# A hybrid decoder step with a mixture of experts: the first expert pair's tokens picked by products of high and low parts of x's rows, kept where the last three weight slots are loaded

## The chip, the cores and the metric

The kernel runs on one core of a Trainium2 chip. The metric is the device time of one execution in microseconds (us); lower is better. Times of several executions are compared by their median.

## The reference, cut to what matters

One layer of a decoder is computed for 256 prompt tokens and 32 sample tokens (8 sequences of 4), so 288 rows of 1024 numbers in float32. Two attention branches and an output projection give new rows `x`; then each row goes through a mixture of 16 experts, of which it uses two:

```python
g_prob = softmax(xn @ w_rg + b_rg); g_p, g_i = top_k(g_prob, 1)
e_logit = (xn @ w_re + b_re).reshape(B, T, 4, 4)          # only the chosen group's 4
e_p, e_i = top_k(softmax(e_logit[g_i]), 2)
w_sel = g_p * e_p / sum(e_p); ids = g_i * 4 + e_i
y = sum over the two experts: w_sel * (silu(xn @ w_gate[e]) * (xn @ w_up[e])) @ w_down[e]
x = x + y; return rms_norm(x, g_final), and the new keys and values
```

## The kernel before, in words

The change lies between the output projection and the experts. The rows of x leave the projection transposed (`xT`, 8 tiles of 128 columns by 288 tokens). `back` adds each tile's part to the router's logits and to the sums of squares in one PSUM bank (`lgp`). `natural(t, c)` (L796) turns token tile t (of 128, 128 and 32 rows), column half c, back into rows: four TensorE transposes into a PSUM bank and one copy into `x2`. `rows_out` writes `x2` to the DRAM tensor `x2_d`, from which POOL later gathers the rows of each expert pair.

VectorE then finds each row's group and two experts (L904 to L926). `cums`, a product with a triangle of ones, numbers the rows of each expert, and `posm` (L939) holds those numbers. An expert has 64 slots, so two experts, a pair, fill 128 slots, and there are eight pairs. One-hot matrices (`oh0` in float32 for pair 0, `onehot` in bfloat16 for pairs 1 to 7) say which row stands in which slot. For pairs 1 to 7 a small product gives row indices (`index_mm`, `index`), and `fetch` gathers the rows from `x2_d` by an indirect DMA. For pair 0 no gather is made: `pick(c)` (L978) multiplies `oh0` with the rows of x2 in SBUF, in float32, which gives `xe0`. `turn_xe` transposes it into `xeT`, scaled by the norm's weights, and the first `gu` product (L1154, gate and up weights) starts. Beside this the same stretch computes row scales for pair 0 (`rsl`, L1022), the combine weights (`cw`), and, inside pair 0's products, `late_router` and `slot_weights`.

The weights of the experts come as 48 loads of 1 MB into a ring of 19 slots in four pools (8, 5, 3 and 3 slots); the loads' order is fixed by `use` (L819). Load n goes to slot n modulo 19. Loads 0 to 15 are issued by SP during the projections. Loads 16 to 18 go to the fourth pool, `rings[3]`, which is allocated when the projection's memory is free: load 16 is issued ahead of the second `rows_out`, loads 17 and 18 behind it (L896 to L903). Load 19 needs slot 0, which the first products of pair 0 set free; from then on each load waits for the products that use the slot's last content. SP issues all of these in program order. Each pair p needs its `gu` products for k from 0 to 3, then k from 4 to 7, and its `pd` products (L1202). The order on PE is written out by a small driver with costs; ACT and VectorE run this stretch in program order (`hold`, L891).

Of the kernel before, what the change touches and what calls it, by code (L numbers as in the profile page):

```python
# [17 lines left out]
D = 1024  # L18
# [103 lines left out]
def build(tc, I, O):  # L122
# [21 lines left out]
    def P(tag, name):  # L144
        return ps.tile([128, 512], F32, tag=tag, name=name, bufs=NBUF[tag])
# [647 lines left out]
            mm(lgp[:n, 72 + t:73 + t], sx[:, t * 128:t * 128 + n], ones[:, 0:1], start=False, stop=last,  # L793
               skip_group_check=True)

    def natural(t, c, copy=nc.scalar.copy):  # L796

        n = TW[t]
        pb = P("at", f"bk{t}{c}")
        for k in range(4):  # L800
            nc.tensor.transpose(pb[:n, k * 128:(k + 1) * 128], xT[c][:, k, t * 128:t * 128 + n], ident)
        copy(x2[:n, t, c * 512:(c + 1) * 512], pb[:n])

    def back(dt, xt, sx):
        if dt == 7:
            natural(0, 0, V.tensor_copy)
            sum_squares(rb, False)
        for t in range(3):
            n = TW[t]
            mm(lgp[:n, t * 24:(t + 1) * 24], xt[:, t * 128:t * 128 + n], wro[:, dt, :], start=(dt == 0 and t == 0),  # L810
               stop=(dt == 7), skip_group_check=True)
        if dt == 7:
            sum_squares(sx, True)
        yield 400.0, 0.0
# [78 lines left out]
    nc.scalar.activation(x2[:, 0:2, D], lgp[:, 72:74], AF.Ln, bias=epst, scale=1.0 / D)  # L893
    nc.scalar.activation(x2[0:32, 2, D:D + 1], lgp[0:32, 74:75], AF.Ln, bias=epst[0:32], scale=1.0 / D)
    nc.scalar.activation(x2[:, :, D], x2[:, :, D], AF.Exp, scale=-0.5)
    for c in range(2):  # L896
        for t in range(c == 0, 3):
            natural(t, c)
        if c:
            ring_loads(1)  # L900
        last = rows_out(slice(c * 512, c * 516 + 512))
    with tc.issue_after(last.ins):
        ring_loads(RINGS[3] - 1)  # L903
    for t in range(3):  # L904
        n = TW[t]
        V.scalar_tensor_tensor(lg[:n, t, :], lgp[:n, t * 24:(t + 1) * 24], x2[:n, t, D:D + 1], br[:n],
# [32 lines left out]
    V.scalar_tensor_tensor(posm, cums[:, 0:48].rearrange("p (t e) -> p t e", e=16), 1.0, OHs, op0=ALU.add, op1=ALU.mult)  # L939


    oh0 = mo.tile([128, 3, 2, CAP], F32, tag="PT", name="oh0", bufs=2)
    onehot = [mo.tile([128, 16, CAP], BF16, tag="y" + "hhl"[t], name=f"oneh{t}", bufs=2) for t in range(3)]
    inv = wk.tile([128, 8], I32, name="inv")
    invf = wk.tile([128, 8], F32, name="invf")
# [8 lines left out]
                        cc("io64")[:, None, :].broadcast_to([128, e1 - e0, CAP]), op=ALU.is_equal)  # L954

    def slots_of(t, pr):
        if pr == 0:
            return oh0[:TW[t], t].rearrange("p e s -> p (e s)")
        return onehot[t][:TW[t], 2 * pr:2 * pr + 2, :].rearrange("p e s -> p (e s)")

    def index_mm(p0, p1):
        for pr in range(p0, p1):
            for t in range(3):
                mm(piv[:, pr, :], slots_of(t, pr), (tokb if pr else tokf)[:TW[t], t, :], start=(t == 0), stop=(t == 2))

    def index(p0, p1):
        rs = slice(p0, p1)
# [7 lines left out]
                                            bounds_check=NT - 1, oob_is_err=False)  # L975


    def pick(c):  # L978
        po = P("at", f"xe0{c}")
        cs = slice(c * 512, c * 512 + 512)  # L980
        for t in range(3):
            mm(po, slots_of(t, 0), x2[:TW[t], t, cs], start=(t == 0), stop=(t == 2))
        (nc.scalar.copy, V.tensor_copy)[c](xe0[:, cs], po)

    def turn_xe(xeT, xe, pr):

        xv = xe[:, 0:D].rearrange("t (p k) -> t k p", k=8)
        for kk in range(2):
            pv = P("at", f"xe{pr}{kk}").rearrange("p (k t) -> p k t", k=4)
            for k in range(4):  # L990
                nc.tensor.transpose(pv[:, k, :], xv[:, 4 * kk + k, :], ident)  # L991
            ks = slice(4 * kk, 4 * kk + 4)
            i = V.tensor_mul(xeT[:, ks, :], pv, gpk[:, ks, None].broadcast_to([128, 4, 128]))  # L993
        return i

    for t in range(3):
        V.tensor_tensor(oh0[:, t], posm[:, t, 0:2, None].broadcast_to([128, 2, CAP]),
                        cc("io64")[:, None, :].broadcast_to([128, 2, CAP]), op=ALU.is_equal)
    for t in range(3):
        mark(t, 2, 6)  # L1000


    ge, gs, ee, es, w2, s4 = s3("ge", 4), s3("gs"), s3("ee", 2), s3("es"), s3("w2", 2), s3("s4")
# [14 lines left out]
    V.reciprocal(gs, gs)  # L1018
    V.reciprocal(s4, s4)
    V.tensor_tensor(ee, ee, bc(s4[:, :, None], 2), op=ALU.mult)  # L1020
    for t in range(3):
        mm(pi[:, 16:17], slots_of(t, 0), x2[:TW[t], t, D:D + 1], start=(t == 0), stop=(t == 2))  # L1022
    xe0 = gt.tile([128, 4 * NT], F32, tag="xT", name="xe0")
    pick(0)
    index_mm(0, 3)
    index(0, 3)
    fetch(1)
    fetch(2)
    pick(1)
    xeTs[0] = gt.tile([128, 4 * NT], F32, tag="xT", name="xeT0")[:, 0:D].rearrange("p (k t) -> p k t", k=8)  # L1030
    rsl[0] = mo.tile([128, 1], F32, tag="rsl", name="rsl0", bufs=3)
    V.tensor_copy(rsl[0], pi[:, 16:17])
    turn_xe(xeTs[0], xe0, 0)
    V.tensor_reduce(es, ee, axis=AX.X, op=ALU.add)
    V.reciprocal(es, es)
    V.tensor_tensor(ee, ee, bc(gs[:, :, None], 2), op=ALU.mult)
# [4 lines left out]
    for t in range(3):  # L1041
        mark(t, 6, 16)
# [5 lines left out]
    def late_router():  # L1048
        for t in range(3):
# [94 lines left out]
    def up(pr):  # L1144
        pt = P("mm", f"gu{pr}")
        if pr == 6:
            gfb.append(ring_slot(52, "gfb")[:, 0:D])
            nc.sync.dma_start(gfb[0], I["g_final"][None, :].broadcast_to([128, D]))
        for k in range(8):
            if pr == 7 and k == 0:  # L1150
                add_rows(1)
                add_rows(0)
            for i in range(2):
                mm(pt[64 * i:64 * i + 64, :], xeTs[pr][:, k, 64 * i:64 * i + 64], W[pr, k // 4, i][:, :, k % 4, :],  # L1154
                   start=(k == 0), stop=(k == 7))
            if pr == 0 and k == 4:
# [5 lines left out]
            if pr == 0 and k == 7:  # L1162
# [204 lines left out]
```

## Time and profile before

| what | value |
| --- | --- |
| time, median of 3 runs | 415.95 us (412.25 to 420.18) |
| time of the profiled execution | 413.99 us, of which 412.2 us span |
| mean granted TensorE clock | 0.989 |
| busy PE, VectorE, ACT, POOL | 95%, 50%, 44%, 23% |
| moved by DMA | 111.12 MB, mean 270 GB/s |

The span is the time from the first to the last instruction; about 1.8 us of the execution lie outside. PE is shown busy nearly always, but a matmul's end is modelled, so that share does not tell how close PE is to its limit. The chain of waits follows the work that ended last back to its causes. DMA share is the mean busy share of 16 DMA engines; GB/s is what they moved.

### The profile page before, as it was taken

The numbers are of one execution on the slowest core, as the hardware profiler recorded it, in microseconds if no ns is written. First come the engines' busy times: TensorE is split into PE (matmuls) and PEld (weight loads), VectorE is DVE, ScalarE is ACT, GpSimd is POOL, SyncE is SP. The second block draws the span as 40 slices with busy tenths as digits, with TensorE's granted clock in tenths as the row PEclk, the third lists the DMA queues.
The fourth block names the chain that finished last, engine by engine and source line by source line (L and its number), as shares of the span: only waits on it lengthen the run. The fifth ranks groups of instructions, "written<-read, shape, count | busy, mean of one in ns | idle before, by whom it ended". The sixth has DMA issues, their size and how long they took to land.

```text
span 412.2 us, 7107 instructions
## 1 busy us (share of the span) xinstructions
PE 393.2 (95%) x2706; PEld 293.5 (71%) x2706; DVE 207.9 (50%) x435; ACT 179.6 (44%) x349; POOL 94.3 (23%) x127
## 2 busy tenths in 40 slices
PE   7899999999999999999999999998999999999990
PEld 4799988858987977997999999984543333333350
DVE  3964468556543647134647785244540111126874
ACT  4854358577653664674554446232001111112353
POOL 3730222105343320610000232331002222033011
PEclk9999999999999999999999999999899999999997
DMA  8998636635743963663899999939599999999903
GB/s 263 327 355 277 222 103 230 223 118 205 260 158 91 338 235 103 220 240 103 192 381 395 341 324 389 409 88 303 189 313 413 410 416 412 417 414 410 343 32 122
DMA packets 56777, 111.12 MB, mean 270 GB/s; under 512 B 7621, under 2 KB 36941, under 8 KB 54689
## 3 DMA queue, kind: packets, MB, share of 16 engines
q1 hardware_dynamic: 49312, 86.56, 59.6%
q0 software_dynamic: 7120, 23.95, 15.8%
q8 instruction: 23, 0.38, 0.4%
q10 hardware_dynamic: 304, 0.09, 0.1%
q14 instruction: 18, 0.14, 0.1%
HBM read 104.72 MB, written 7.43 MB: 272 GB/s over the span
## 4 chain that ended last, share of the span: by engine, by line
PE 69%; DMA 20%; ACT 3%; issue 2%; DVE 2%; POOL 1%; SPq 1%; DVEq 0%; POOLq 0%
DMA w<-in_w_expert_up 15%; PE g L347 10%; PE g L351 10%; PE g L348 10%; DMA w<-in_w_expert_down 6%; PE gu L1154 4%; PE pk L616 3%; PE p L347 2%; PE p L348 2%; PE p L351 2%; PE ss L622 2%; PE o L347 2%; PE pos L647 2%; PE pd L1202 2%; PE po L588 2%
## 5 line engine op out<-in xcount | busy, mean ns | idle before, releaser
L347 PE MATMUL g<-xTh,hi 128*128 128x288 f32 x312 | 90.7, 311 | 0.0
L348 PE MATMUL g<-xTl,hi 128*128 128x288 f32 x312 | 85.7, 296 | 0.0
L1154 PE MATMUL gu<-w,xeT 128*64 128x512 f32 x256 | 62.0, 612 | 1.1 <-DMA w<-in_w_expert_up 0.7
L347 PEld LDWEIGHTS g<-xTh,hi 128*128 128x128 f32 x312 | 58.7, 188 | 1.0 <-issue 0.9
L348 PEld LDWEIGHTS g<-xTl,hi 128*128 128x128 f32 x312 | 58.9, 189 | 0.0
L351 PE MATMUL g<-xTh,li 128*128 128x288 f32 x312 | 50.5, 300 | 0.0
L333 DVE TENSOR_TENSOR li<-rawi,hi 128x1024 fp32r<-128x1024 f32 x39 | 47.3, 1215 | 3.0 <-ACT hi L328 3.0
L328 ACT CAST hi<-rawi 128x1024 fp32r<-128x1024 f32 x39 | 40.8, 1049 | 15.2 <-PE g L348 15.1
L351 PEld LDWEIGHTS g<-xTh,li 128*128 128x128 f32 x312 | 43.8, 189 | 1.7 <-issue 1.7
L1154 PEld LDWEIGHTS gu<-w,xeT 128*64 128x64 f32 x256 | 18.7, 139 | 33.1 <-issue 31.4
L1202 PE MATMUL pd<-w,hT 128*64 128x512 f32 x128 | 29.2, 598 | 0.0
L993 DVE TENSOR_TENSOR xeT<-xe,gpk 128x512 f32<-128x512 f32 x16 | 10.4, 686 | 22.9 <-PE xe L991 22.9
L617 ACT COPY KT<-pk 128x512 f32<-128x512 f32 x30 | 18.6, 639 | 7.1 <-PE pk L616 6.7
L1172 DVE SCALAR_TENSOR_TENSOR h<-gu,rsl,h 128x256 f32<-128x256 f32 x8 | 3.9, 484 | 34.3 <-ACT h L1169 34.3
L973 POOL DMA_INDIRECT xe<-x_d,inv x7 | 7.3, 1041 | 56.7 <-DVE rsl L1141 26.2
L1169 ACT ACTIVATE h<-gu,rsl 128x256 f32<-128x256 f32 x8 | 3.8, 474 | 37.5 <-PE gu L1154 19.8
L1202 PEld LDWEIGHTS pd<-w,hT 128*64 128x64 f32 x128 | 8.6, 136 | 15.4 <-issue 13.7
L616 PE MATMUL pk<-blob,kp 128*128 128x128 f32 x128 | 19.4, 274 | 0.1
L505 DVE TENSOR_TENSOR gate<-g,rb 128x288 f32<-128x288 f32 x16 | 7.3, 457 | 21.3 <-PE g L351 21.1
L347 PE MATMUL p<-oTh,hp 128*128 128x288 f32 x64 | 17.5, 296 | 0.0
L348 PE MATMUL p<-oTl,hp 128*128 128x288 f32 x64 | 17.4, 294 | 0.0
L1212 ACT COPY y<-pd 128x512 f32<-128x512 f32 x10 | 5.9, 586 | 23.6 <-PE pd L1202 23.6
(301 smaller groups left out, 708.6 us busy)
## 6 DMA issues: line engine op xcount, KB each, us to landing
rawi<-in_w_in SPq DMA_DIRECT2D x19, 1024.0 KB
w<-in_w_expert_gate SPq DMA_DIRECT2D x32, 512.0 KB
w<-in_w_expert_up SPq DMA_DIRECT2D x32, 512.0 KB
w<-in_w_expert_down SPq DMA_DIRECT2D x16, 1024.0 KB
rawo<-in_w_out SPq DMA_DIRECT2D x4, 1024.0 KB
y_d<-y POOLq DMA_DIRECT2D x10, 256.0 KB, 9.6
rawp<-in_w_proj_sb SPq DMA_DIRECT2D x2, 1024.0 KB
rawp<-in_w_proj_moba SPq DMA_DIRECT2D x2, 1024.0 KB
```

The costliest lines, as they stand in the source:

```text
L328: nc.scalar.copy(h, src)
L333: V.tensor_sub(l, src, h.bitcast(F32))
L347: mm(o, h[:, k, :], mh[k], start=(k == 0), stop=False)
L348: mm(o, h[:, k, :], ml[k], start=False, stop=False)
L351: mm(o, l[:, k, :], mh[k], start=False, stop=(k == n - 1))
L588: mm(po[64 * s:64 * s + 64, 128 * c:256], vn[:, c, h * 64:(h + 1) * 64], aT[s][:, 256 * c:256 + 128 * c], start=(c == 0), stop=(c == 1))
L616: nc.tensor.transpose(pv[:, j, :], kp[:, c, j * 128:(j + 1) * 128], ident)
L617: nc.any.tensor_copy(kt[:, :, c:256:2], pv)
L622: mm(pt[32 * bb:32 * bb + 32, 0:260], Qb[:, j, 4 * G + bb, :, :].rearrange("p h q -> p (h q)"), KT[bb][:, j, :], start=(j == 0), stop=(j = ...
L993: i = V.tensor_mul(xeT[:, ks, :], pv, gpk[:, ks, None].broadcast_to([128, 4, 128]))
L1154: mm(pt[64 * i:64 * i + 64, :], xeTs[pr][:, k, 64 * i:64 * i + 64], W[pr, k // 4, i][:, :, k % 4, :], start=(k == 0), stop=(k == 7))
L1202: mm(pd[64 * i:64 * i + 64, :], hT[:, k, 64 * i:64 * i + 64], W[pr, 2, i][:, k, c * 512:(c + 1) * 512], start=(k == 0), stop=(k == 1))
```

## The change

The rows of x are stored twice more for pair 0's pick: a high part (a cast to fp32r, `xsp[t][:, 0]`) and a low part (row minus high part, `xsp[t][:, 1]`). These three tiles take the three slots of `rings[3]`, so loads 16 to 18 are issued behind the last product that reads them. `pick` becomes six fp32r products per column half in place of three in float32. The first `natural` moves from VectorE to ACT and behind the logits; ACT writes two copies for each. The low parts are computed by POOL for column half 0, by VectorE for half 1. Pair 0's indices are no longer computed, its row scales move into `late_router`, the one-hot matrices of pairs 3 to 7 are computed ahead of the combine weights, `late_router` moves from k = 4 to k = 5 of pair 0, and `slot_weights` from pair 0 to pair 1.

```diff
+        nc.scalar.copy(xsp[t][:n, 0, cs], pb[:n])
+        nc.scalar.copy(x2[:n, t, cs], pb[:n])
+
+    def natural_low(t, c, eng):
...
+        eng.tensor_sub(xsp[t][:n, 1, cs], x2[:n, t, cs], xsp[t][:n, 0, cs].bitcast(F32))
...
         if dt == 7:
-            natural(0, 0, V.tensor_copy)
             sum_squares(rb, False)
...
+    xsp = [rings[3].tile([128, 2, D], F32R, tag="w", name=f"xsp{t}") for t in range(3)]
     for c in range(2):
-        for t in range(c == 0, 3):
+        for t in range(3):
             natural(t, c)
-        if c:
-            ring_loads(1)
-        last = rows_out(slice(c * 512, c * 516 + 512))
-    with tc.issue_after(last.ins):
-        ring_loads(RINGS[3] - 1)
+            if c == 0:
+                natural_low(t, c, nc.gpsimd)
+        rows_out(slice(c * 512, c * 516 + 512))
...
     def pick(c):
         po = P("at", f"xe0{c}")
         cs = slice(c * 512, c * 512 + 512)
-        for t in range(3):
-            mm(po, slots_of(t, 0), x2[:TW[t], t, cs], start=(t == 0), stop=(t == 2))
-        (nc.scalar.copy, V.tensor_copy)[c](xe0[:, cs], po)
+        for j in range(2):
+            for t in range(3):
+                mm(po, oh0_of(t), xsp[t][:TW[t], j, cs], start=(j == 0 and t == 0), stop=(j == 1 and t == 2))
+        if c == 0:
+            nc.scalar.copy(xe0[:, cs], po)
+        else:
+            nc.scalar.copy(xe0[:, 512:768], po[:, 0:256])
+            V.tensor_copy(xe0[:, 768:1024], po[:, 256:512])
...
+    natural_low(0, 1, V)
+    natural_low(1, 1, V)
+    natural_low(2, 1, V)
     for t in range(3):
         mark(t, 2, 6)
+    xe0 = gt.tile([128, 4 * NT], F32, tag="xT", name="xe0")
+    pick(0)
+    pick(1)
+    ring_loads(RINGS[3])
+    index_mm(1, 3)
+    index(1, 3)
+    fetch(1)
+    fetch(2)
...
+    turn_xe(xeTs[0], xe0, 0)
+    for t in range(3):
+        mark(t, 6, 16)
```

On SP's queue, before, load 16 (`w_3412`) stands ahead of the four writes of x, loads 17 and 18 (`w_3417`, `w_3420`) behind them, and load 19 (`w_3647`) waits for PE:

```order
L850 DMA w_3412<-in_w_expert_gate 128x1024 [waits DMAHW6_49,PE_49,Activation_49]
L850 DMA w_3412<-in_w_expert_up 128x1024 [waits DMAHW7_49]
L787 DMA x_d<-x_2650 128x2x512 [waits DMAHW0_49,DVE_49,Activation_49]
L788 DMA x_d<-x_2650 32x512 [waits DMAHW1_49,Activation_49]
L787 DMA x_d<-x_2650 128x2x516 [waits DMAHW2_49,Activation_49]
L788 DMA x_d<-x_2650 32x516 [waits DMAHW3_49,Activation_49]
L850 DMA w_3417<-in_w_expert_gate 128x1024 [waits DMAHW4_49]
L850 DMA w_3417<-in_w_expert_up 128x1024 [waits DMAHW5_49]
L850 DMA w_3420<-in_w_expert_down 128x2048 [waits DMAHW6_49]
L850 DMA w_3647<-in_w_expert_down 128x2048 [waits DMAHW7_49,PE_49]
```

Now, at the same place of SP's queue (loads 16 to 18 are `w_3500`, `w_3503` and `w_3506`, load 19 is `w_3656`):

```order
L787 DMA x_d<-x_2650 128x2x512 [waits DMAHW6_49,Activation_49]
L788 DMA x_d<-x_2650 32x512 [waits DMAHW7_49,Activation_49]
L787 DMA x_d<-x_2650 128x2x516 [waits DMAHW0_49,Activation_49]
L788 DMA x_d<-x_2650 32x516 [waits DMAHW1_49,Activation_49]
L856 DMA w_3500<-in_w_expert_gate 128x1024 [waits DMAHW2_49,PE_49,Pool_49]
L856 DMA w_3500<-in_w_expert_up 128x1024 [waits DMAHW3_49]
L856 DMA w_3503<-in_w_expert_gate 128x1024 [waits DMAHW4_49,PE_49,Pool_49]
L856 DMA w_3503<-in_w_expert_up 128x1024 [waits DMAHW5_49]
L856 DMA w_3506<-in_w_expert_down 128x2048 [waits DMAHW6_49,PE_49,Pool_49]
L856 DMA w_3656<-in_w_expert_down 128x2048 [waits DMAHW7_49,PE_49]
```

All four writes of x now stand ahead of the three loads, and each of these waits for PE and POOL where it waited for neither.

On POOL, before, between the clearing of two gather buffers (`xe`) and the first gather:

```order
L886 DMA y_d<-xe_3366 16x1024 [waits Pool_49]
L888 IOTA ioi 128x384 [waits PE_49,Activation_49]
L890 CAST io_3373<-ioi 128x384 [waits Pool_49]
L973 DMA xe_3367<-x_d,inv 128x1028 [waits DMAHW2_49,DMAHW1_49,DMAHW3_49,DMAHW0_49,DVE_49]
L973 DMA xe_3366<-x_d,inv 128x1028 [waits DMASW0_49]
```

And now, where `xsp` are the split rows and `x_2650` is x2:

```order
L892 DMA y_d<-xe_3360 16x1024 [waits Pool_49]
L894 IOTA ioi 128x384 [waits PE_49,Activation_49]
L809 TENSOR_TENSOR xsp_3374<-x_2650,xsp_3374 128x512 [waits Activation_49]
L896 CAST io_3367<-ioi 128x384 [waits Pool_49]
L809 TENSOR_TENSOR xsp_3375<-x_2650,xsp_3375 128x512 [waits Activation_49]
L809 TENSOR_TENSOR xsp_3376<-x_2650,xsp_3376 32x512 [waits Activation_49]
L976 DMA xe_3361<-x_d,inv 128x1028 [waits DMAHW6_49,DMAHW1_49,DMAHW7_49,DMAHW0_49,DVE_49]
L976 DMA xe_3360<-x_d,inv 128x1028 [waits DMASW0_49]
```

Three subtractions came in ahead of the gathers, one of them ahead of the cast.

## Rows read from the trace of the kernel before

**Rows 1.** The page's second part: what the DMA engines moved in 40 equal slices of the span

```profile
GB/s 263 327 355 277 222 103 230 223 118 205 260 158 91 338 235 103 220 240 103 192 381 395 341 324 389 409 88 303 189 313 413 410 416 412 417 414 410 343 32 122
```

**Rows 2.** The chain of waits from 270 us on: start us, us, what

```profile
271.49 1.07 PE o L351 x8
272.57 0.44 PE bk L801 x4
...
368.11 20.14 DMA w<-in_w_expert_up
...
388.39 3.62 PE gu L1154 x14
```

**Rows 3.** Waits of PE, 300 to 395 us: waited for, us, times, longest

```profile
PE gu L1154 <- DMA w<-in_w_expert_up: 0.7, 1, 0.7
```

**Rows 4.** Stretches: length, busy PE PEld DVE ACT POOL, clock, DMA share, GB/s

```profile
268.60:274.90 6.30, 6.30 (x54) 6.11 (x53) 1.59 (x3) 0.89 (x2) 3.06 (x4) 1.00 0.05 18
275.00:276.00 1.00, 1.00 (x11) 0.95 (x11) 0.50 (x4) 0.97 (x4) 0.87 (x2) 1.00 0.39 61
274.00:288.00 14.00, 13.12 (x69) 7.75 (x68) 6.37 (x46) 5.37 (x13) 2.91 (x5) 1.00 0.89 255
274.00:308.00 34.00, 32.02 (x172) 17.26 (x173) 17.21 (x86) 6.22 (x15) 5.00 (x7) 0.95 0.79 247
302.00:308.00 6.00, 6.00 (x37) 2.90 (x37) 1.91 (x10) 0.84 (x2) 1.00 (x1) 1.00 0.89 243
290.00:294.00 4.00, 3.77 (x10) 1.78 (x12) 3.86 (x12) 0.00 (x0) 0.00 (x0) 0.57 0.48 179
320.00:388.00 68.00, 67.46 (x317) 24.41 (x316) 20.20 (x37) 12.95 (x24) 13.57 (x17) 1.00 1.02 403
```

**Rows 5.** SP's timeline, 274 to 297 us: start us, us, queue, line, DMA

```profile
274.98 0.33 SPq L850 DMA_DIRECT2D w<-in_w_expert_gate  x1
...
278.05 1.84 SPq L788 DMA_DIRECT2D x_d<-x  x1
...
281.80 14.13 SPq L850 DMA_DIRECT2D w<-in_w_expert_down  x2
296.03 0.38 SPq L850 DMA_DIRECT2D w<-in_w_expert_gate  x1
```

**Rows 6.** Timeline of the routing stage, 274.9 to 290.5 us

```profile
275.54 2.49 ACT L802 COPY x<-bk 128x512 f32<-128x512 f32 x5
...
276.81 0.21 DVE L916 TENSOR_TENSOR el<-blob,gi 128x48 f32<-128x48 f32 x1
...
279.37 0.70 DVE L997 TENSOR_TENSOR oh<-posm,blob 128x128 f32<-128x128 f32 x3
...
279.98 1.09 DVE L953 TENSOR_TENSOR oneh<-posm,blob 128x256 bf16<-128x256 f32 x3
...
280.56 3.03 PE L982 MATMUL xe<-x,oh 128*128 128x512 f32 x6
...
284.85 3.03 PE L982 MATMUL xe<-x,oh 128*128 128x512 f32 x6
...
287.01 1.06 POOL L973 DMA_INDIRECT xe<-x_d,inv  x1 [10.93 <-DMA x_d<-x]
...
288.76 1.13 PE L991 MATMUL xe<-blob,xe 128*128 128x128 f32 x8 [0.88 <-DVE rsl L1032]
...
290.23 1.04 PE L1154 MATMUL gu<-w,xeT 128*64 128x512 f32 x2 [0.33 <-DMA w<-in_w_expert_down]
```

**Rows 7.** Timelines of POOL and VectorE, 8 us and 229 to 234 us

```profile
8.36 1.28 POOL L240 TENSOR_TENSOR xTl<-xg,xTh 128x512 fp32r<-128x512 f32 x1 [5.90 <-ACT xTh L236]
...
229.90 1.22 DVE L333 TENSOR_TENSOR lp<-rawp,hp 128x1024 fp32r<-128x1024 f32 x1
...
233.05 0.81 POOL L716 TENSOR_TENSOR gate<-gate,gate 128x288 f32<-128x288 f32 x1 [0.67 <-DVE gate L715]
233.07 1.87 DVE L333 TENSOR_TENSOR lp<-rawp,hp 128x1024 fp32r<-128x1024 f32 x1
```

More of the change, by code (lines that the diff above doesn't have):

```diff
@@ L794, in sum_squares, with natural @@
                skip_group_check=True)
-    def natural(t, c, copy=nc.scalar.copy):
+    def natural(t, c):
         n = TW[t]
+        cs = slice(c * 512, (c + 1) * 512)
         pb = P("at", f"bk{t}{c}")
@@ L801, in natural @@
             nc.tensor.transpose(pb[:n, k * 128:(k + 1) * 128], xT[c][:, k, t * 128:t * 128 + n], ident)
-        copy(x2[:n, t, c * 512:(c + 1) * 512], pb[:n])
+        nc.scalar.copy(xsp[t][:n, 0, cs], pb[:n])
+        nc.scalar.copy(x2[:n, t, cs], pb[:n])
+    def natural_low(t, c, eng):
+        n = TW[t]
+        cs = slice(c * 512, (c + 1) * 512)
+        eng.tensor_sub(xsp[t][:n, 1, cs], x2[:n, t, cs], xsp[t][:n, 0, cs].bitcast(F32))
     def back(dt, xt, sx):
         if dt == 7:
-            natural(0, 0, V.tensor_copy)
             sum_squares(rb, False)
@@ L939, in build @@
     V.scalar_tensor_tensor(posm, cums[:, 0:48].rearrange("p (t e) -> p t e", e=16), 1.0, OHs, op0=ALU.add, op1=ALU.mult)
-    oh0 = mo.tile([128, 3, 2, CAP], F32, tag="PT", name="oh0", bufs=2)
+    oh0 = mo.tile([128, 3, 2, CAP], F32R, tag="PT", name="oh0", bufs=2)
     onehot = [mo.tile([128, 16, CAP], BF16, tag="y" + "hhl"[t], name=f"oneh{t}", bufs=2) for t in range(3)]
@@ L956, in slots_of @@
     def slots_of(t, pr):
-        if pr == 0:
-            return oh0[:TW[t], t].rearrange("p e s -> p (e s)")
         return onehot[t][:TW[t], 2 * pr:2 * pr + 2, :].rearrange("p e s -> p (e s)")
@@ L963, in index_mm @@
             for t in range(3):
-                mm(piv[:, pr, :], slots_of(t, pr), (tokb if pr else tokf)[:TW[t], t, :], start=(t == 0), stop=(t == 2))
+                mm(piv[:, pr, :], slots_of(t, pr), tokb[:TW[t], t, :], start=(t == 0), stop=(t == 2))
     def index(p0, p1):
@@ L975, in fetch, with oh0_of @@
                                             bounds_check=NT - 1, oob_is_err=False)
+    def oh0_of(t):
+        return oh0[:TW[t], t].rearrange("p e s -> p (e s)")
     def pick(c):
@@ L991, in turn_xe @@
                 nc.tensor.transpose(pv[:, k, :], xv[:, 4 * kk + k, :], ident)
-            ks = slice(4 * kk, 4 * kk + 4)
-            i = V.tensor_mul(xeT[:, ks, :], pv, gpk[:, ks, None].broadcast_to([128, 4, 128]))
+            for a, b in (((0, 2), (2, 4)) if pr == 0 and kk == 0 else ((0, 4),)):
+                ks = slice(4 * kk + a, 4 * kk + b)
+                i = V.tensor_mul(xeT[:, ks, :], pv[:, a:b, :], gpk[:, ks, None].broadcast_to([128, b - a, 128]))
         return i
@@ L998, in build @@
                         cc("io64")[:, None, :].broadcast_to([128, 2, CAP]), op=ALU.is_equal)
+    natural_low(0, 1, V)
+    natural_low(1, 1, V)
+    natural_low(2, 1, V)
     for t in range(3):
         mark(t, 2, 6)
+    xe0 = gt.tile([128, 4 * NT], F32, tag="xT", name="xe0")
[6 more added lines that the diff above has]
+    fetch(2)
+    xeTs[0] = gt.tile([128, 4 * NT], F32, tag="xT", name="xeT0")[:, 0:D].rearrange("p (k t) -> p k t", k=8)
+    rsl[0] = mo.tile([128, 1], F32, tag="rsl", name="rsl0", bufs=3)
+    turn_xe(xeTs[0], xe0, 0)
+    for t in range(3):
+        mark(t, 6, 16)
     ge, gs, ee, es, w2, s4 = s3("ge", 4), s3("gs"), s3("ee", 2), s3("es"), s3("w2", 2), s3("s4")
@@ L1020, in build @@
     V.tensor_tensor(ee, ee, bc(s4[:, :, None], 2), op=ALU.mult)
[L1021 to L1033, printed above, removed]
     V.tensor_reduce(es, ee, axis=AX.X, op=ALU.add)
@@ L1040, in build @@
     V.tensor_add(cw, cw, tmp)
-    for t in range(3):
-        mark(t, 6, 16)
     V.tensor_copy(cw3[:, :, :, 0], cw)
@@ L1048, in late_router @@
     def late_router():
+        for t in range(3):
+            mm(pi[:, 16:17], oh0_of(t).bitcast(F32), x2[:TW[t], t, D:D + 1], start=(t == 0), stop=(t == 2))
+        V.tensor_copy(rsl[0], pi[:, 16:17])
         for t in range(3):
@@ L1155, in up @@
                    start=(k == 0), stop=(k == 7))
-            if pr == 0 and k == 4:
+            if pr == 0 and k == 5:
                 late_router()
@@ L1161, in up @@
                     fetch(pr + 3)
-            if pr == 0 and k == 7:
+            if pr == 1 and k == 5:
                 slot_weights()
```

## The prediction, on record before the result was known

> **What bounds the kernel now.** I read the page's slices first. In the slices from 309 to 381 us the DMA engines move 410 to 417 GB/s, and in the four slices ahead of that 88 to 313 [rows 1]. The chain of waits says the same from the other end: its last long piece is a load of gate and up weights that was issued at 368.11 us and landed 20.14 us later, at 388.25, and right behind it come the last expert products [rows 2]. PE's own waits show how narrow this is: between 300 and 395 us it waited for weights once, for 0.7 us [rows 3]. So two things end almost together: the stream of weights, and PE, which has eight pairs to work through. To end earlier both must move; to end later, one is enough.
>
> The stream's end is its amount over its rate plus the time in which the DMA engines were idle or slow. The stretches show where that is [rows 4]. Full rate is 403 GB/s (320 to 388 us). From 268.6 to 274.9 us there are 18 GB/s, since 16 loads are out and the next slots are not free. From 274 to 308 us the mean is 247 GB/s, so 34 x (1 - 247/403) = 13.2 us of full flow are lost there. SP's timeline gives the reason for one part: load 16 goes out at 274.98, the last write of x at 278.05, load 18 at 281.80, and then the queue stands until load 19 finds slot 0 free; its row merges two loads over 14.13 us, and load 20 follows at 296.03 [rows 5]. Slot 0 comes free when pair 0's first products are done, and they begin only at 290.23 [rows 6]. The timeline of the stage shows what stands ahead of them: two picks in float32, 3.03 us each, with the indices between, then transposes at 288.76.
>
> **The change, part by part: the way to the first expert product.** All sums are made on the profiled execution, 413.99 us, of which the span is 412.2; it lies 0.5% under the median of 415.95.
>
> The four transposes of natural(0, 0) leave the way to the logits: 0.44 us on the chain [rows 2], so ACT's row copies start at 275.54 - 0.44 = 275.1 [rows 6].
>
> ACT makes 12 copies in place of 5. Five took 2.49 us [rows 6], some 0.49 each, so 12 take 5.9 and end at 281.0; the last x2 copy of half 0 is done at 278.1. Before, all of them were done at 278.0. So the first write of x is issued at 278.1, the second at 281.1.
>
> POOL makes three subtractions of 512 columns. Its row for that shape and type shows 1.28 us [rows 7]. The first can start when the first x2 copy is there, at about 276.25, and with the cast between (0.5) the three end at 280.6 if nothing holds POOL up. They lie beside VectorE's routing chain, and that is what I worry about. The rows show it: a VectorE subtraction of 1024 columns from SBUF takes 1.22 us alone, and 1.87 us when it starts 0.02 us behind a POOL operation of 0.81 us [rows 7]; it waited 0.65, nearly until POOL was done. The routing chain has five short operations with two operands in SBUF (L916, L917, two of L925, L926); the first took 0.21 us at 276.81 [rows 6], so it comes up at about 276.4 now. No row shows such short ones beside POOL. If they wait for nothing, `oh0` is ready at 279.9 (before: 280.07 by 279.37 + 0.70 [rows 6]; the chain starts 0.44 earlier, but the PE work ahead of `cums` has grown by a transpose group). If each waits for the POOL operation it meets, I step through it: the first waits from 276.4 to 277.5, the next 0.5 for the cast, the next until the second subtraction ends at 279.65, the next until the third ends at 281.05. Then `cums`, `posm` and `oh0` follow as before, and `oh0` is ready at about 282.8. I take this end, since the row of the long operation shows a wait that lasts to the end.
>
> The Trainium skill ("SBUF — State Buffer", section "SBUF: two separate sides") says that VectorE and GpSimd share a pair of SBUF ports under an exclusive lock, held for the whole instruction, for VectorE operations with two SBUF inputs too. By that the short ones wait as well and the sum stays as it is; without it the picks would end 2.2 us earlier. The row of 1.87 us agrees with it, for a long operation.
>
> The picks: eight fp32r products of 288 columns take 1.07 us in the chain [rows 2], 0.13 each, so 512 columns should take 0.13 x 512/288 = 0.23 us, and twelve 2.8 us, against 2 x 3.03 = 6.06. Behind `oh0` VectorE makes three low parts of 0.6 each (half of 1.22), until 284.6, and the last product follows at 285.0. Unhindered it would be 282.8. I call this moment T.
>
> Behind T: VectorE's three `mark`s, 1.09 us [rows 6], stand ahead of its quarter copy of `xe0`; then four transposes (half of 1.13), half a scaling, and the first `gu` starts near 287.1, 3.1 us earlier than 290.23. The row scales (now in `late_router`) and the later combine weights leave this way; `late_router` grows by three small products, behind which `gu` continues; PE has the time, as the DMA sum below shows.
>
> **The change, part by part: the weight stream.** The bytes are the same, so only lost time counts, from 274 us on, against the 13.2 us of before.
> - Start. Load 16 no longer goes out at 274.98. The first traffic is the write of x, issued at 278.1. The load of before needed about 1.2 us to flow (275 to 276 us: 61 GB/s [rows 4]), so the engines are idle until 279.3: 5.3 us lost.
> - Writes of x, 1.1 MB. From 274 to 288 us the mean is 255 GB/s [rows 4], 5.1 us lost, of which about 1.9 are the empty start; 3.2 us I put down to the writes, and they come again. In the old order they were done at 287.01, when the first gather began [rows 6]; now they run from 279.3 to about 285.
> - Gap until loads 16 to 18 flow, T + 1.2 = 286.2: 1.1 us (none if T is 282.8).
> - Loads 16 to 18 are 3.1 MB and with two gathers of 0.5 MB last until 296. Load 20 followed 5.8 us behind the first `gu` (296.03 less 290.23), and load 19 just ahead of it, so slot 0 is free near 292.5; load 19 comes in time and the weak stretch of before (290 to 294 us, DMA share 0.48 [rows 4]) goes.
> - 302 to 308 us: 243 GB/s, 2.4 us lost [rows 4], when few loads are in flight. With loads already queued I count half, 1.2.
>
> Sum: 5.3 + 3.2 + 1.1 + 1.2 = 10.8 us, against 13.2: the stream ends 2.4 us earlier, at 385.9. PE is 3.1 us earlier, so it waits about 1.4 us for the last weights where it waited 0.7, and the tail behind (PE, VectorE, output) is unchanged. So 413.99 - 2.4 = 411.6; with the same difference the median goes from 415.95 to 413.6.
>
> The bounds: with T = 282.8 and nothing lost at 302 to 308, 8.5 us are lost, a gain of 4.7. With T at 287.6 (below) and all of the 2.4, 14.6 are lost: 1.4 us slower.
>
> **Rivals.**
> 1. The lock does not touch the short operations. For it: no row shows them waiting. Against it: the row of 1.87. Then T = 282.8 and the gain is 4.7 at most: 411.3 on the median.
> 2. Slower: the three loads wait on a pick that runs at half clock. If the routing chain waits for POOL, PE stands for some 3 us between the second half's transposes (done at 277.7; one warming product follows until 278.5) and `cums` (281.5). In the old trace the granted clock fell to 0.57 in 290 to 294 us, behind gaps around 288 and 290 [rows 4]. At half clock twelve picks cost 2.6 us more, T is 287.6, and the loads begin 3.7 us behind the writes of x: 14.6 us lost with the whole of 302 to 308, so +1.4: 417.4. It decides from T = 287.3 on at my other terms: there the stream breaks even, and each further us of T costs one. Against it: warming products stand on both sides of `cums`, and from 274 to 288 us PE is shown busy for 13.12 of 14 us at full clock [rows 4], with the first of them in it.
> 3. PE's wait for the last weights grows enough to lower the clock, and the last products, 3.62 us at full clock [rows 2], start slow. The stretch of 290 to 294 us shows the price: 4 us at 0.57 lose 1.7. Then the net is -0.7: 415.3. For it: with both gains at their best PE would wait 3 to 4 us there. Against it: at my numbers it is 1.4.
>
> **How the numbers follow.** Forecast 0.45, rival 1 0.2, rival 2 0.2, rival 3 0.15. All of them lie within 2% (8.3 us), which is about what a measurement of this kernel can tell from no change; the three runs before lie 3.7 us under and 4.2 over their median. The likeliest is 413.6 us. The cases reach from 411.3 to 417.4; with a median of few runs off by some 3 us I take 408 to 420. For faster by over 2% the stream would have to lose almost nothing in front: 0.05. For slower by over 2% T would have to slip by another 7 us beyond rival 2: 0.04. Within: 0.91.
>
> **What would show it.** Right: `gu` starts at 286 to 288 us; SP issues load 16 behind the last pick, at about 285; no stretch without DMA between that and 385; the last gate and up load lands 2 to 3 us earlier; PE waits for it 1 to 2 us. VectorE's short operations lengthened to 0.5 to 1.3 us beside POOL's subtractions would show the lock. Wrong: a `gu` start before 285 (rival 1), a clock near 0.5 during the picks and a hole in the DMA row at 285 to 288 (rival 2), or a landing later than 388 us.

## The result, and the profile after the change

The changed kernel takes 418.02 us (median of 16 executions, 414.03 to 420.79), the kernel before 415.19 us (16 executions, 412.25 to 420.18): ratio 1.0057, 95% interval 1.0033 to 1.0081. So it is 0.6% slower, and the forecast had the sign wrong: 2.4 us less were predicted, 2.8 more came, within its range of 408 to 420. The profiled execution takes 418.36 us with a span of 416.6, against 413.99 and 412.2 before. The ratios leave out executions more than 1.5% above the fastest of their kernel, five of the changed kernel's sixteen here; the medians of all sixteen give 1.0068.

This execution is 1.2 us late before it reaches the change: the last projection products of the chain start at 272.71 us, where [rows 2] have 271.49. All times below are to be read with that 1.2 us in mind.

The stage of the change on the timeline (start, duration, engine, line, operation; in brackets the idle time ahead and what ended it); [rows 6] and [rows 7] are its counterpart:

```profile
277.60 1.27 POOL L809 TENSOR_TENSOR xsp<-x,xsp 128x512 fp32r<-128x512 f32 x1 [0.93 <-ACT x L804]
277.72 1.22 DVE L921 TENSOR_TENSOR el<-blob,gi 128x48 f32<-128x48 f32 x1
...
278.82 0.50 POOL L896 CAST io<-ioi 128x384 f32<-128x384 int32 x1
...
278.97 0.41 DVE L922 SCALAR_TENSOR_TENSOR el<-el,lg 128x48 f32<-128x48 f32 x1
...
279.28 2.48 POOL L809 TENSOR_TENSOR xsp<-x,xsp 128x512 fp32r<-128x512 f32 x2
...
280.21 1.62 DVE L930 TENSOR_TENSOR OH<-blob,ei 128x48 f32<-128x48 f32 x2
...
282.12 0.17 PE L941 MATMUL cums<-OHs,trib 128*128 128x16 bf16 x1 [2.26 <-DVE OHs L931]
...
282.81 0.70 DVE L1009 TENSOR_TENSOR oh<-posm,blob 128x128 fp32r<-128x128 f32 x3
...
283.39 8.02 PE L989 MATMUL xe<-xsp,oh 128*128 128x512 f32 x12
...
294.23 5.85 PE L1170 MATMUL gu<-w,xeT 128*64 128x512 f32 x24
```

VectorE's L921 starts 0.12 us behind POOL's first subtraction and lasts 1.22 us, where the same work took 0.21 in [rows 6]; both end at 278.9. L922 meets the cast and ends with it, at 279.3; the two operations of L930 stand until POOL's last subtraction is done, at 281.8. TensorE (PE) has nothing from 279.86 to 282.12, and then the twelve picks take 8.0 us.

The same stretch in windows (busy time of PE, PEld, DVE, ACT, POOL; then granted clock, DMA share, GB/s), to be held against [rows 4]:

```profile
280.00:282.00 2.00, 0.00 (x0) 0.00 (x0) 1.93 (x6) 2.00 (x5) 1.76 (x2) 0.90 0.55 191
282.00:295.00 13.00, 12.47 (x36) 6.42 (x37) 5.91 (x19) 1.26 (x3) 1.88 (x2) 0.50 0.39 114
284.00:291.00 7.00, 7.00 (x13) 2.97 (x11) 2.31 (x6) 0.59 (x1) 0.00 (x0) 0.50 0.00 0
274.00:308.00 34.00, 30.95 (x152) 16.50 (x151) 21.03 (x88) 10.02 (x23) 9.87 (x11) 0.80 0.60 217
```

From 282 to 295 us the granted clock is 0.50, that is 1.2 GHz in place of 2.4, and in seven of these microseconds the DMA engines move nothing at all. SP's queue says why (against [rows 5]):

```profile
282.32 0.32 SPq L788 DMA_DIRECT2D x_d<-x  x1
290.33 0.34 SPq L856 DMA_DIRECT2D w<-in_w_expert_gate  x1
```

The writes of x are out at 282.3, and the next load waits for the picks until 290.33. (Before, load 16 was not free of engines either: in the order of SP's queue it waits for PE and ACT, and it went out at 274.98; loads 17 and 18 waited for no engine.) Over 274 to 308 us the mean is 217 GB/s, before it was 247 [rows 4]. The end of the chain and PE's last wait for weights ([rows 2], [rows 3]):

```profile
272.71 1.09 PE o L351 x8
...
372.72 20.16 DMA w<-in_w_expert_up
```

```profile
393.01 3.62 PE L1170 MATMUL gu<-w,xeT 128*64 128x512 f32 x14 [1.73 <-DMA w<-in_w_expert_up]
```

The last up weights land at 392.88, before at 388.25: 4.6 us later, 3.4 of them beyond the late start. PE waits for them 1.73 us, before 0.73. What follows them is as long as before.

### The profile page after: what moved, and what is told of

The parts are those of the page before. It is cut to its first block, busy times and chain, and to the rows that moved or that the text cites. A ratio compares the mean times of both kernels' runs of the same rounds, so it can differ in the third digit from the quotient of the medians.

```text
span 416.6 us, 7111 instructions
## 1 busy us (share of the span) xinstructions
PE 397.4 (95%) x2700; PEld 296.8 (71%) x2700; DVE 210.9 (51%) x438; ACT 183.3 (44%) x357; POOL 98.5 (24%) x130
## 4 chain that ended last, share of the span: by engine, by line
PE 71%; DMA 20%; DVE 3%; ACT 2%; issue 2%; SPq 0%; DVEq 0%
DMA w<-in_w_expert_up 15%; PE g L347 10%; PE g L351 10%; PE g L348 9%; DMA w<-in_w_expert_down 4%; PE gu L1170 4%; PE pk L616 3%; PE p L347 2%; PE p L348 2%; PE p L351 2%; PE ss L622 2%; PE o L347 2%; PE pos L647 2%; PE pd L1218 2%; PE xe L989 2%; PE po L588 2%
## 5 line engine op out<-in xcount | busy, mean ns | idle before, releaser
L1170 PE MATMUL gu<-w,xeT 128*64 128x512 f32 x256 | 60.7, 602 | 1.7 <-DMA w<-in_w_expert_up 1.7
L1170 PEld LDWEIGHTS gu<-w,xeT 128*64 128x64 f32 x256 | 17.6, 138 | 33.8 <-issue 31.6
L1005 DVE TENSOR_TENSOR xeT<-xe,gpk 128x512 f32<-128x512 f32 (+1 forms) x17 | 10.6, 656 | 22.1 <-PE xe L1002 22.0
L616 PEld LDWEIGHTS pk<-blob,kp 128*128 128x128 f32 x128 | 15.3, 141 | 0.7 <-DVE t L520 0.3
```

Source lines behind the costliest of these rows:

```text
L616: nc.tensor.transpose(pv[:, j, :], kp[:, c, j * 128:(j + 1) * 128], ident)
L1005: i = V.tensor_mul(xeT[:, ks, :], pv[:, a:b, :], gpk[:, ks, None].broadcast_to([128, b - a, 128]))
```

## The experiments

The theory of the lock: GpSimd's subtractions hold VectorE's short routing operations, PE stands empty ahead of the prefix products, and the clock falls for the picks on which three loads wait. The rival: what costs is that three loads wait for the picks at all. Later experiments ask where the clock is lost; the letters in an expectation are its own. A warming product is a product whose result nothing reads; it only gives PE something to do, and "fed" in the table means that such products were put into PE's waits. Each ratio is against the kernel before on the same chip. The clock in the table is the median over the executions that the comparison uses; that of the kernel before was 0.989 to 0.991 in the four sets.

| kernel | ratio (95%) | clock |
|---|---|---|
| the change | 1.0057 (1.0033 to 1.0081) | 0.977 |
| low parts all on VectorE | 0.9967 (0.9933 to 1.0002) | 0.986 |
| the change, four warming products | 1.0028 (0.9995 to 1.0062) | 0.987 |
| before, lock alone | 1.0212 (1.0175 to 1.0249) | 0.979 |
| before, late loads | 1.0072 (1.0031 to 1.0114) | 0.986 |
| the same, released earlier | 1.0088 (1.0059 to 1.0117) | 0.985 |
| low parts on VectorE, two slots | 1.0004 (0.9980 to 1.0028) | 0.985 |
| the same as line 2, fed at the end | 0.9985 (0.9953 to 1.0016) | 0.983 |
| the same as line 2, fed in front | 0.9992 (0.9958 to 1.0026) | 0.987 |
| late loads released earlier, fed at the end | 1.0043 (0.9999 to 1.0087) | 0.982 |
| before, fed | 0.9941 (0.9911 to 0.9970) | 0.992 |
| low parts on VectorE, high parts first, fed | 0.9950 (0.9917 to 0.9984) | 0.990 |

**The lock taken away.** The three low parts of the first half move from GpSimd to VectorE, behind `oh0`:

```diff
-            if c == 0:
-                natural_low(t, c, nc.gpsimd)
...
+    for t in range(3):
+        natural_low(t, 0, V)
     natural_low(0, 1, V)
```

> The changed kernel, but VectorE makes the low parts of column half 0 too, behind oh0, so that POOL does nothing beside the routing chain. Theory A (POOL's subtractions hold VectorE's routing chain up by 2.6 us, PE stands for 2.3 us, its clock falls to half and the picks take 7.2 us): the chain's operations take 0.2 to 0.3 us again, PE's gap ahead of cums is under 1 us, the granted clock is 1.0 during the picks, the last pick ends near 285 us and the first gu starts near 287.5; the time is 3 to 5 us under the changed kernel's, at 413 to 415. Rival B (the late loads of slots 16 to 18 are the loss, whatever the clock): gu starts earlier but the time stays within 1.5 us of 418. Rival C (fp32r products of 512 columns are slow at any clock): the clock is 1.0 and the picks still take 7 us.

Measured: 412.77 us, ratio 0.9967. Its timeline and two stretches:

```profile
278.22 0.21 DVE L919 TENSOR_TENSOR el<-blob,gi 128x48 f32<-128x48 f32 x1
...
279.50 0.33 DVE L928 TENSOR_TENSOR OH<-blob,ei 128x48 f32<-128x48 f32 x2
...
282.40 4.76 PE L987 MATMUL xe<-xsp,oh 128*128 128x512 f32 x12
```

```profile
276.00:280.00 4.00, 4.00 (x23) 3.72 (x23) 2.91 (x27) 3.39 (x9) 1.67 (x4) 0.57 0.12 20
296.00:300.00 4.00, 4.00 (x24) 2.21 (x24) 0.93 (x7) 0.00 (x0) 0.00 (x0) 0.62 1.02 422
```

The two routing lines are short again, 0.21 and 0.33 us, with no POOL operation beside them, and the picks take 4.76 us at full clock. The change without its GpSimd part is not slower than before: taking the lock away turns a loss into none. The clock still falls, here from 276 to 280 us with PE shown busy throughout, and again behind 296.

**The hole filled, the lock kept.** `warm(1, 416)` ahead of the prefix products becomes `warm(4, 416)`.

> The changed kernel with four warming products in place of one ahead of cums, three more in the gap in which PE stands; POOL's subtractions stay where they are. Theory A: the routing chain is as slow as in the changed kernel (its first long operation 1.2 us again), but the clock stays at 1.0, twelve picks take 3 to 4 us instead of 7.2, the first gu starts 3 to 5 us earlier than 294.2 and the time is 414 to 415.5. Rival B: the clock stays up, and the time stays near 418. Rival C: the clock stays up and the picks still take 7 us.

Measured: 414.48 us, ratio 1.0028, clock 0.987 in place of 0.977. Timeline and stretch:

```profile
276.15 1.22 DVE L921 TENSOR_TENSOR el<-blob,gi 128x48 f32<-128x48 f32 x1
...
277.44 2.96 PE L195 MATMUL warm<-rst 128*128 128x416 f32 x8
...
281.66 4.39 PE L989 MATMUL xe<-xsp,oh 128*128 128x512 f32 x12
```

```profile
276.00:296.00 20.00, 18.91 (x101) 10.66 (x99) 15.31 (x55) 7.44 (x16) 6.22 (x6) 1.00 0.63 219
```

L921 still takes 1.22 us, so the lock stands; four warming products cover the hole, and the picks run at full clock, twelve in 4.39 us, 0.37 each. The ratio lies between those of the change and of the first experiment, and its interval touches both; the part that the clock has is shown by the granted clock rather than by the time.

**The lock alone, in the kernel before.** Three subtractions whose result nothing reads, on GpSimd at the place of the change's; loads and float32 picks as before:

```diff
+            if c == 0:
+                for t in range(3):
+                    n = TW[t]
+                    nc.gpsimd.tensor_sub(xes[1][:n, 0:512], x2[:n, t, 0:512],
+                        xT[0].rearrange("p k t -> p (k t)")[:n, 0:512])
```

> The kernel before, float32 picks and early loads, and three subtractions of 512 columns on GpSimd at the place where the change has them, whose result nothing uses: the lock alone, without late loads. Theory A: VectorE's short routing operations with two SBUF operands take 1.2 to 1.6 us instead of 0.2 to 0.3, oh0 is ready about 2.3 us later, TensorE stands some 2 us ahead of the prefix products and the granted clock falls towards 0.5 for the first pick; gu starts 3 to 5 us later and, as slot 0 comes free that much later, load 19 too: 2 to 4 us slower, ratio 1.005 to 1.010. Rival: the weights ahead of load 19 are in flight anyway and the later gu is caught up, ratio 0.999 to 1.003, although the clock falls.

> The run with the lock alone once more, for a trace of another execution: five of its six executions took 418.4 to 423.7 us at a granted clock of 0.965 to 0.985, and the one with a trace 415.0 at 0.990. If this one is of the longer kind, some 15 to 17 us at half clock must stand in one or more places: by theory B at 280 to 300 us, behind TensorE's hole of 1.7 us ahead of the prefix products; by theory A behind 386 us.

Measured: ratio 1.0212, far above the expected 1.005 to 1.010 (six executions from 415.0 to 423.7 us), and 421.96 us in one more execution, with a span of 420.2 where the first trace had 413.2. The two traces are of one and the same program; first the one of 415.02 us, timeline and stretches:

```profile
276.72 1.20 DVE L921 SCALAR_TENSOR_TENSOR el<-el,lg 128x48 f32<-128x48 f32 x1
...
279.67 0.17 PE L940 MATMUL cums<-OHs,trib 128*128 128x16 bf16 x1 [2.30 <-DVE OHs L930]
...
281.52 4.68 PE L986 MATMUL xe<-x,oh 128*128 128x512 f32 x6
...
287.46 3.04 PE L986 MATMUL xe<-x,oh 128*128 128x512 f32 x6
...
297.01 0.38 SPq L850 DMA_DIRECT2D w<-in_w_expert_gate  x1
```

```profile
282.00:295.00 13.00, 11.72 (x42) 5.45 (x42) 4.89 (x24) 2.33 (x5) 2.07 (x2) 0.87 0.75 231
295.00:300.00 5.00, 5.00 (x36) 2.56 (x34) 3.50 (x14) 0.00 (x0) 0.00 (x0) 1.00 0.45 159
```

Then the one of 421.96 us:

```profile
279.41 0.17 PE L940 MATMUL cums<-OHs,trib 128*128 128x16 bf16 x1 [2.31 <-DVE OHs L930]
...
281.68 5.78 PE L986 MATMUL xe<-x,oh 128*128 128x512 f32 x6
...
289.36 5.78 PE L986 MATMUL xe<-x,oh 128*128 128x512 f32 x6
...
303.63 0.38 SPq L850 DMA_DIRECT2D w<-in_w_expert_gate  x1
```

```profile
282.00:295.00 13.00, 13.00 (x24) 4.90 (x23) 1.17 (x9) 2.22 (x5) 2.06 (x2) 0.50 0.71 218
295.00:300.00 5.00, 4.12 (x15) 2.52 (x16) 3.31 (x12) 0.00 (x0) 0.00 (x0) 0.50 0.03 8
```

VectorE and the hole are alike in both, 2.30 and 2.31 us of empty PE. What differs is the clock behind it. In the first execution it is at half for 3.4 us (13 x (1 - 0.87) / 0.5), the two picks take 4.68 and 3.04 us and load 19 is issued at 297.01. In the second it stays at 0.50 until 301 us, both picks take 5.78, load 19 goes out at 303.63, and the DMA engines stand nearly still from 295 to 300. The 7 us between the spans are accounted for by the 6.6 us between the two issues of load 19. So the lock costs without any late load: the half clock reaches the weight stream through slot 0, which the first pair frees.

**Late loads alone.** Float32 picks and no GpSimd work, but loads 16 to 18 wait for writes into their slots. These writes stand behind the second pick's copy in the first kernel, behind the indices in the second:

```diff
+    held_slots = [rings[3].tile([128, 2048], F32, tag="w", name=f"hs{t}") for t in range(3)]
...
+    for t in range(3):
+        V.memset(held_slots[t][:, 0:1], 0.0)
+    ring_loads(RINGS[3])
```

> The kernel before, with loads 16 to 18 held back until the second pick's copy is done (three tiles stand in their slots and are written by one short operation each); picks in float32 as before. Theory A: by the sum of lost DMA time, 13.8 us against 13.2, the time is 0 to 1.5 us over the kernel before. Rival B: the late loads alone cost what the whole change costs, 2.4 us or more.

> As the run in which only the three loads of the kernel before were made late, but the slots are released by three writes of VectorE behind the indices instead of behind the second pick's copy: the loads go out at about 285.4 instead of 288.7. By the sum over the DMA engines the stream then loses 3 us less than in that run: theory A, the cost is in proportion to the time without weights in flight, expects 0.998 to 1.002 of before (that run: 1.007). Rival B: the order alone costs (writes of x first, weights behind them, their use bunched up), whatever the moment: 1.005 to 1.008 again.

Measured: 416.25 us (1.0072) and 415.40 us (1.0088). Two stretches of the second kernel's trace:

```profile
281.00:287.00 6.00, 6.00 (x23) 2.67 (x22) 1.71 (x15) 2.33 (x5) 1.06 (x1) 1.00 0.04 8
274.00:308.00 34.00, 32.02 (x180) 17.22 (x181) 18.08 (x91) 6.22 (x15) 5.21 (x7) 1.00 0.73 261
```

The hole in the DMA row is there (8 GB/s, in the first kernel 1), and the loads go out at 285.75, in the first kernel at 288.74. By the DMA sum the second stream is even ahead of the old one, 261 against 247 GB/s over 274 to 308 us, and its last weights land at 388.0 us. Three microseconds of earlier loads bought nothing in the medians: the cost is not in proportion to the time without weights, and the rival is right in this much, that late loads alone cost 0.7 to 0.9% under float32 picks. Both traces are of executions with a high clock (0.993 and 0.995), the quickest of their kernels; the median clocks, 0.986 and 0.985, are lower than that of the kernel before. Why late loads should go with a lower clock is open. But the clock is not all of their cost: the executions with a clock of 0.989 or more take 415.8 and 414.8 us by the median (three of each kernel), those of the kernel before 412.2 to 412.6.

**Load 16 early again.** As the first experiment, but the rows of the last 32 tokens stand in the two gather buffers, and only two slots wait.

> The low parts all made by VectorE behind oh0 as in the experiment that moved them there, and of the three weight slots only two hold the split rows (the rows of the last 32 tokens stand in the two gather buffers, which are cleared behind the picks), so load 16 goes out where the kernel before has it, ahead of the writes of x, and only loads 17 and 18 wait for the picks. Theory A (each microsecond without weights in flight costs its share of the stream): load 16's 1 MB, 2.6 us at 403 GB/s, fills the hole ahead of the writes, so the stream ends some 2 us earlier than with all three late; that run stood at 0.997 of before, this one at 0.990 to 0.995, 410 to 412 us by its chip's 413.7. Rival B (what costs is that loads stand behind the picks at all, one or three): as the run with all three late or worse, 0.997 to 1.003. Rival C (PE's work, not the stream, ends it): no change against the run with all three late, 0.997, with PE waiting for no weights at the end.

Measured: 412.84 us, ratio 1.0004. Stretches:

```profile
276.00:285.00 9.00, 8.59 (x47) 5.24 (x47) 7.49 (x38) 7.00 (x16) 0.95 (x2) 1.00 0.73 248
274.00:308.00 34.00, 33.16 (x183) 17.82 (x184) 21.95 (x94) 10.40 (x24) 7.37 (x9) 0.95 0.78 263
```

248 GB/s flow from 276 to 285 us, where the first experiment had 141, and over 274 to 308 us it is 263 against 243. The trace has that gain at the end too (last weights at 387.5, there 389.0), the median has not: 0.990 to 0.995 was expected from the time without weights, and 1.0004 came. The clock of this execution is at 0.57 from 286 to 290 us.

**Where the clock goes.** Two warming products in PE's wait for the last weights, once on the first experiment, once on the late loads; and the router's narrow products dealt out behind three column blocks, with two small warming products in PE's waits:

```diff
             for i in range(2):
+                if pr == 7 and k == 4 and i == 1:
+                    warm(2, 416)
                 mm(pt[64 * i:64 * i + 64, :], xeTs[pr][:, k, 64 * i:64 * i + 64],
```

> The run with all low parts on VectorE, plus two warming products of 416 columns (1.7 us) in TensorE's wait for the last up weights (1.6 us in that run's trace), between the two experts' products of pair 7's fifth column block. Question: where do the runs that no trace shows lose their clock? That run's mean granted clock over its executions is 0.986, that of the kernel before 0.990 (1.7 us more at half clock's price). Theory A (my third rival: the longer wait for the last weights lowers the clock of what follows it): the clock goes to 0.989 or more and the time 1 to 1.5 us under that run, ratio 0.992 to 0.995. Theory B (the clock is lost in the routing stage and behind it, 276 to 300 us): clock and ratio stay, 0.986 and 0.997, or 0.1 us worse by the products.

> The run with only the loads late, released behind the indices (1.009 of before, mean clock 0.985, though its trace showed 0.995 and a wait of 1.97 us for the last weights), plus two warming products of 416 columns in that wait. Theory A (the wait lowers the clock behind it): clock 0.990 or more and ratio 1.000 to 1.004. Theory B: clock 0.985 and ratio 1.009 as before.

> The run with all low parts on VectorE, with the router's narrow products (row scales, counts and indices, 2.5 us in one piece at 294.7 us of its trace, ahead of 3.4 us at half clock) dealt out behind three column blocks of the first pair in place of one, and two warming products of 208 columns in TensorE's two short waits (ahead of and behind the transposes of xe). Theory B (clock lost in the routing stage and behind it): clock 0.988 to 0.991 in place of 0.986, time 1 to 2 us under that run: ratio 0.991 to 0.995. Theory A (lost at the stream's end): no change, 0.997.

Measured: 0.9985 at a clock of 0.983, 1.0043 at 0.982, 0.9992 at 0.987. Stretches of the first:

```profile
282.00:290.00 8.00, 7.60 (x29) 3.65 (x30) 6.12 (x21) 1.06 (x5) 2.06 (x2) 0.57 0.79 252
384.00:388.00 4.00, 4.00 (x14) 1.29 (x12) 3.96 (x6) 2.03 (x3) 0.00 (x0) 1.00 1.01 384
```

Of the late loads fed at the end:

```profile
284.00:295.00 11.00, 10.12 (x24) 4.19 (x25) 4.81 (x19) 0.00 (x0) 2.06 (x2) 0.54 0.81 275
388.00:392.00 4.00, 4.00 (x16) 1.34 (x15) 3.96 (x6) 2.03 (x3) 0.00 (x0) 1.00 0.99 402
```
In both PE is never empty at the end (4.00 of 4 us) and its clock there is 1.00; it is at half at 282 to 290 us, at 284 to 295 us. So in these traces the clock is lost in the routing stage and the first pair, and feeding the end does not raise the median clock; that 1.0043 lies under 1.0088 the intervals do not secure. Dealing out the narrow products missed as well: in its trace 294 to 302 us is at 0.57, and the time is that of the first experiment within the intervals.

**The holes of the stage filled.** First in the kernel before: two warming products in place of one ahead of the prefix products, one of 416 columns behind the second pick, one of 208 behind the transposes of `xe`. Then in the first experiment's kernel: the six products of high parts first, and a small warming product ahead of each low one:

```diff
+    pick_high(0)
+    pick_high(1)
...
         for t in range(3):
+            again(1, 160)
             mm(po, oh0_of(t), xsp[t][:TW[t], 1, cs], start=False, stop=(t == 2))
```

> The kernel before with TensorE's holes of the routing stage filled by warming products: two of 416 columns in place of one ahead of the prefix products (hole of 0.8 us), one of 416 columns behind the second pick (hole of 0.9 us) and one of 208 behind the transposes of xe. The weights and the routing are as before. If the clock is lost behind holes, the mean clock goes from 0.990 to 0.992 or more and the time 1 to 2 us down: ratio 0.995 to 0.998. If narrow products lower it as well as holes, nothing changes: 0.999 to 1.002.

> The run with all low parts on VectorE, with the picks' six products of high parts first (they wait for no low part) and a warming product of 160 columns ahead of each of the six of low parts, which VectorE hands over every 0.62 us, and one of 208 columns behind the indices. The end of the picks is set by VectorE's low parts as in that run. If what lowers the clock there is a TensorE that is shown busy but waits inside (0.40 us per product where 0.23 is its pace elsewhere), the mean clock goes from 0.986 to 0.990 and the ratio from 0.997 to 0.990 to 0.994. If not, 0.997 again, or 0.5 us worse by the products.

Measured: 411.37 us (0.9941, clock 0.992) and 411.68 us (0.9950, clock 0.990). Both beat the kernel before, and they cannot be told from each other. The second on the timeline and in a stretch:

```profile
280.03 2.21 PE L993 MATMUL xe<-xsp,oh 128*128 128x512 f32 x6
...
288.18 5.44 PE L1186 MATMUL gu<-w,xeT 128*64 128x512 f32 x24
```

```profile
278.00:300.00 22.00, 21.84 (x124) 12.96 (x123) 15.77 (x57) 5.93 (x13) 2.10 (x3) 1.00 0.77 280
```

Six products of high parts take 2.21 us, 0.37 each, the first pair starts at 288.18, and the clock is 1.00 from 278 to 300; ahead of that, over 274 to 278 us, it is at 0.57. The repaired change is no faster than the repaired old kernel.

The same trace shows where the 0.37 us come from. Here the products of low parts stand one by one between pairs of warming records, and the chain of waits counts them singly (L1000 at 283.21 has 128 rows of weights, at 283.71 it is the third token tile, with 32):

```profile
283.21 0.23 PE xe L1000
283.44 0.27 PE warm L944 x2
283.71 0.43 PE xe L1000
284.14 0.47 PE warm L944 x2
```

A product of 128 rows takes the 0.23 us that were forecast. The one of 32 rows takes 0.20 more, and so do the warming products behind it. In the trace with four warming products the load of the 32-row weights begins at 282.30 us, together with its product, while that of the second 128-row product begins 0.2 us ahead of it (281.77 and 281.97). So every third product is paid for going in and coming out: 4 x (3 x 0.23 + 2 x 0.20) = 4.4 us for twelve, as measured.

Of the fed kernel before the trace caught its longest execution (416.69 us), PE's timeline and two stretches:

```profile
389.21 5.31 PE L1162 MATMUL gu<-w,xeT 128*64 128x512 f32 x14 [2.18 <-DMA w<-in_w_expert_up]
```

```profile
284.00:288.00 4.00, 4.00 (x9) 1.57 (x9) 0.39 (x3) 0.00 (x0) 2.06 (x2) 0.57 0.96 232
388.00:392.00 4.00, 2.79 (x10) 1.08 (x12) 3.93 (x5) 1.34 (x2) 0.00 (x0) 0.74 0.90 368
```

Here PE waited 2.18 us for the last weights, the clock fell (0.74 over 388 to 392), and the last 14 products took 5.31 us in place of 3.62 [rows 2]. So my third rival exists; it was seen once. The stage still fell to 0.57 at 284 to 288 us.

## Why the prediction was wrong

- **The copies and the writes of x: right.** ACT's twelve copies were to end at 281.0, with the late start 282.2; they end at 282.3. The second half's write, forecast for 281.1 (282.3), goes out in two parts at 281.36 and 282.32.
- **The lock: right, and nearly to its size.** Stepped through the POOL operations, `oh0` was to be ready at 282.8 (284.0 with the late start); it is at 283.5. The Trainium skill ("SBUF — State Buffer", section "SBUF: two separate sides") has the shared port pair held for a whole instruction, for VectorE operations with two SBUF inputs too. The trace agrees for short operations: 1.22 us in place of 0.21. The first rival, no lock, falls.
- **The picks: wrong, and this is the step that failed.** "512 columns should take 0.13 x 512/288 = 0.23 us, and twelve 2.8 us". They take 0.37 each at full clock (4.39 us for twelve in the second experiment), which is 1.6 us more, and 0.60 to 0.67 at half clock (7.2 us in the chain, 8.0 on the timeline), some 3 us more again. The forecast took its 0.13 from products of 128 rows and left out that each third pick has 32: that is the 1.6 us, by the chain of the last experiment. So T, the end of the last pick, was not 285.0 (286.2 with the late start) but 291.4, and the first `gu`, forecast for 287.1, started at 294.23. In the trace with four warming products the last pick ends 4.1 us behind `oh0`, which for `oh0` at 282.8 puts T at 286.9, and the prediction's own sum breaks even at 287.3. By that sum the third tile alone uses up nearly all of the gain, and the half clock makes the loss.
- **The clock: the mechanism was named, at too low a chance and too small a size.** Rival 2 got 0.2 because of the warming products on both sides of `cums`. The hole between them, forecast at 3 us, is 2.26, and behind it the clock is at half for some 13 us, not for the picks alone. Rival 2 had +1.4 us with T at 287.6 (288.8); it came out at +2.8 on the medians. Its signs are what came: a clock of 0.50 during the picks and a hole in the DMA row.
- **The weight stream: wrong by what T is late.** A gap of 1.1 us was forecast until the three loads flow; the hole is 7 us (284 to 291). By the sum of the prediction 34 x (1 - 217/403) = 15.7 us are lost in 274 to 308 us, where 10.8 were forecast and 14.6 under rival 2; some 1.2 of the 15.7 is the late start. With T at 290.2 in place of 285.0 the sum gives a gap of 6.4, so 5.3 + 3.2 + 6.4 + 1.2 = 16.1 us lost and a time 2.9 us longer, and the medians differ by 2.8. That this fits so well is luck: in the trace only some 14.5 us are lost, 1.3 more than before, and yet the last weights land 3.4 us later. PE's wait at the end, forecast at 1.4, is 1.73.
- **The sum itself is in doubt too.** The late loads alone cost 2.6 and 2.8 us by the medians, where the sum of lost DMA time gives 0.6 (13.8 against 13.2) or less; releasing them 3 us earlier, or load 16 early again, moved the stream and not the time. With the hole filled and the picks at full clock the change shows no gain (1.0028). Without the lock it gives 0.3%, or 1.4 us by 0.0033 x 413.69, with an interval from 2.8 us to none; the forecast's 2.4 us are not shown by any run.

How much of it is clock? An estimate: by a straight line through the executions compared, a hundredth less of mean clock costs 2.1 us in the change, 2.4 in the first experiment and 2.7 to 3.6 in the kernel before. The change has 0.977 and the first experiment 0.986, so the clock is worth some 2 us of the 3.7 between them (0.9% of 415). The rest is then delay: the routing chain's, and that of the loads behind it. Executions at 0.989 or more agree, though those of the change are only two: the kernel before 412.2 to 412.6 us by the medians of four sets (62 executions), the first experiment 412.2 (3), the two fed kernels 411.2 (11 and 7), the change 414.5 (2).

Open: what decides in a given execution whether the clock falls and for how long, why late loads go with a lower one, and what they cost besides the clock.

## What to carry to other kernels

Work given to GpSimd beside a chain of short VectorE operations can hold each of them that reads two operands from SBUF until the GpSimd operation beside it is done (0.21 us became 1.22 here; the operations with one such operand, MAX8 at 0.33, kept their time), and the price is paid again by the engine that waits at its end. A product's price is to be read from rows with the same number of weight rows, and from its neighbours too. Where PE stands empty ahead of products that everything waits for, work out those products at both levels of the clock and give the lower level its full chance; a warming product in each hole cost little and brought 0.6% here. One trace is one execution: list the granted clock of all of them before a difference of a per cent is explained from a trace.

## What was not expected

- One program, two executions: 415.0 and 422.0 us, with 3.4 and 20 us at half clock behind the same hole, while PE is shown busy for 13.00 of 13 us in the longer one.
- The clock also falls without a hole: 0.57 from 276 to 280 us in the first experiment, with PE busy for 4.00 of 4 us on transposes, behind narrow products of 1 and 24 columns.
- Twelve fp32r products of 512 columns take 0.37 us each, although one takes 0.23: every third has 32 rows of weights, and each change of the number of rows cost 0.2 us.
- The kernel before had 0.6% to gain from three more warming products.
